# Moving four things in a layer's order of instructions: h's low parts, later column sums, the values' parts, and two stores

## The chip, the cores and the metric

The kernel runs on one core of a Trainium2 chip. The metric is the device time of one launch in microseconds (us); it is measured in several runs, and one execution was profiled besides. The engines are called PE (TensorE), DVE (VectorE), ACT (ScalarE), POOL (GpSimd) and SP (SyncE, which here issues DMA transfers).

## The reference

One layer of a diffusion transformer over 2048 rows of 1024, with 256 rows of context. Everything is fp32.

```python
h  = _modulate(_rmsnorm(x, norm1_g), sh1, sc1)      # h * (1 + sc1) + sh1
hc = _modulate(_rmsnorm(xc, norm1_g), csh1, csc1)
rq, rk, rv, rg, aq, ak, av = jnp.split(h @ w_in, SPLIT_IDX, axis=-1)
...
ret, _, _ = _bidir_retention(rq_h, rk_h, _heads(rv, RET_HEADS), log_gamma, s_f, s_b)
ret = _ret_out(ret, rg, ret_gn_g)                   # norm, then a gate of silu(rg)
...
att = _latent_attention(q..., k, v, kc, vc)         # 8 heads of 64, 2 heads of keys and values
x = x + g1 * (jnp.concatenate([ret, att], axis=-1) @ w_out)
h2 = _modulate(_rmsnorm(x, norm2_g), sh2, sc2)
x = x + g2 * _sqrelu_mlp(h2, w_ff1, w_ff2)
return _rmsnorm(x, final_norm_g)
```

The retention runs over 16 chunks of 128 rows, forwards and backwards: `state = state * c_dec + (k * k_dec)^T v`. The six vectors sh1 to g2 are 1024 wide each and come from `silu(c) @ w_mod + b_mod`.

## The kernel before

Each fp32 product on PE is made of three fp16 products. An operand is split in a high part, rounded by ACT, and a low part, the difference, by DVE; line 645 multiplies high by high, line 646 high by the weights' low part, line 647 h's low part by the weights' high part.

All of it is one program for five engines with manual order: nothing is reordered behind the author's back, each engine works through its own list, and semaphores make it wait for the others. The order is set by a plan. `at(q, step, fn, ...)` puts a function into half-slot q of the first stage, at one of eight steps, and at the end the plan is emitted half-slot by half-slot, step by step:

```python
STEPS = ("dma", "mm", "turn", "copy", "work", "mix", "extra", "store")
```

A slot is one row tile of 128 rows times one chunk of columns of `w_in`, half a slot is half of it: twelve matmuls of 128x128 by 128x512. The chunks come in the order retention values (rv), retention keys (rk), attention keys and values, attention queries, gates (rg, some 435 to 523 us), retention queries (rq, the last chunk, some 523 to 640 us). `rg` and `rq` also name the first half-slots of these chunks. After that come attention and the output projection (to some 1620 us), whose plan `on(k, phase, fn)` is of the same kind, and last the feed-forward part.

What the change touches:

- In the first chunk h is made tile by tile and half by half: PE transposes (`turn_h`, line 461, tile `psx`, two buffers in PSUM), DVE multiplies by the scale (`modulate`, line 466) and POOL adds the shift (line 467), ACT rounds (`high_h`, line 471), DVE subtracts (`low_h`, line 475). Beside it DVE norms later tiles (line 452) and builds the decay tables (lines 973 to 980).
- `later_rows` makes the vectors that are needed later (gates 1 and 2, shift and scale 2). Slices of `w_mod` are loaded (`wmr`), DVE adds them up weighted into `macc` (lines 381 and 383; one buffer), and PE sums over the partitions with a matrix of ones into `mps` (`sums`, line 388; one buffer). `biases` loads `b_mod`, `whole` adds it.
- `value_parts` finds the greatest attention value (lines 770 to 774), writes it per partition to DRAM and reads it back as a row for all partitions (lines 777 and 780), makes a power of two of it (lines 784 to 789), and splits the values with it (lines 793 to 795).
- `ff_scales` finds in the same manner the scales of the feed-forward part (write line 852, read line 855, `scales` lines 859 to 883, `down_scales` lines 888 to 895, then the output's).
- `forward_states(c, q)` makes the forward state of chunk c. SP loads keys and values (line 1007, two buffers), POOL weighs the keys (line 1012), PE multiplies (`product`, line 1018, in the buffer that `mps` has too), DVE adds to the old state (`update`, line 1027), SP stores. They stand at `rq + 4 + c * 29 // 16`, so most products are two half-slots apart, and 5 and 6, and 10 and 11, are one apart.
- `output_tile(t, ...)` adds the projection to a row tile of x, ACT sums its squares (line 1476), `store_x` stores it (line 1479), POOL norms it in place (line 1489), and PE transposes it (line 1494). The tiles run from 15 down to 0, so t = 1 and t = 0 are the last.

Beside DVE's part in the last chunk stands the rotation of the queries (lines 678 and 693). DMA transfers of all queues share eight rotating semaphores, so a transfer is issued only when the transfer eight before it has landed.

Of the kernel before, what the change touches and what calls it, by code (L numbers as in the profile page):

```python
# [55 lines left out]
def layer_kernel(ctx: ExitStack, tc: tile.TileContext, a: dict, out: bass.AP):  # L56
    nc = tc.nc
# [27 lines left out]
    def scratch(name, n, shape, dtype=F32):  # L85
        return [dram.tile(shape, dtype, name=f"{name}{i}", tag=f"{name}{i}") for i in range(n)]
# [13 lines left out]
    x1_d = scratch("x1", NT, [P, D])  # L100
# [161 lines left out]
    with ExitStack() as st:  # L262
# [26 lines left out]
        def at(q, step, fn, *args):  # L289
            plan.setdefault((q, step), []).append((fn, args))  # L290
# [73 lines left out]
        def later_rows(j, use, qs):  # L364


            x = {}

            def load(i, k):
                w = x[i, k] = sg.tile([P, 2, 512], F32, name="wmr", tag="wmr")  # L370
                src = a["w_mod"][0, k * P : (k + 2) * P, (j + i) * 512 : (j + i + 1) * 512]
                nc.sync.dma_start(w, src.rearrange("(k p) n -> p k n", p=P))

            def add(i, k):
                w = x.pop((i, k))
                if k == 0:
                    x["acc"] = one.tile([P, 512], F32, name="macc", tag="macc")
                for r in range(2):
                    c, acc = cc[:, k + r, :1], x["acc"]
                    if k + r == 0:  # L380
                        nc.vector.tensor_scalar_mul(acc, w[:, r], c)
                    else:
                        nc.vector.scalar_tensor_tensor(acc, w[:, r], c, acc, op0=ALU.mult, op1=ALU.add)

            def sums(i):
                if i == 0:
                    x["ps"] = psM.tile([P, 512], F32, name="mps", tag="mps", bufs=1)
                mm(x["ps"][32 * i : 32 * i + 32], ones, x["acc"], start=True, stop=True)

            def biases():  # L390
                b = x["b"] = op.tile([P, 512], F32, name="mrow", tag="xs", bufs=3)
                for i in range(2):
                    src = a["b_mod"][0, (j + i) * 512 : (j + i + 1) * 512]
                    nc.sync.dma_start(b[32 * i : 32 * i + 32], src.partition_broadcast(32))

            def whole():
                nc.vector.tensor_tensor(x["b"][:64], x["ps"][:64], x["b"][:64], op=ALU.add)

            for n, q in enumerate(qs):
                i, k = n // 4, n % 4 * 2  # L400
                at(q - 3, "dma", load, i, k)
                at(q, "extra", add, i, k)
                if k == KT - 2:
                    at(q + 1, "turn", sums, i)
            at(q, "store", biases)
            at(q + 3, "work", whole)
            use(x, q + 4)

        def store_gate(r):
            def store(x):  # L410
# [66 lines left out]
        def first_turn(m):  # L477

            return 2 * m - (3 if m < 4 else 4 if m < 8 else 5 if m < 12 else 6)

        for m in range(2, len(TILES)):
            q = first_turn(m)
            if m > 3:
                at(max(0, first_turn(m - 4) + 2 if m > 5 else 0), "dma", load_x, m)
            if m > 2:
                at(max(0, q - 3), "copy", squares, m)
                at(max(0, q - 2), "work", root, m)
                at(max(1, q - 1), "mix", normal, m)
            for p in range(2):
                at(q + p, "turn", turn_h, m, p)  # L490
                at(q + p + 1, "work", modulate, m, p)
                at(q + p + 2, "copy", high_h, m, p)
                at(q + p + 2, "copy", low_h, m, p)

        class Weights:

# [259 lines left out]
        def value_parts(q0):  # L756

            x = {}

            def load():  # L760
                nc.vector.memset(wv[:, :, :, HD : HD + 1], 1.0)
                for i in range(3):
                    x[i] = xp.tile([P, 2, 6, HD], F32, name="vn", tag="x")
                    nc.sync.dma_start(x[i], av_d[:, :, 6 * i : 6 * i + 6])
                w = xp.tile([P, P + 8], F32, name="vma", tag="x")
                x["m"], x["r"], x["s"], x["e"] = w[:, :P], w[:, P : P + 4], w[:, P + 4 : P + 5], w[:, P + 5 : P + 6]

            def greatest(i):
                v = x[i].rearrange("p g k d -> p (g k d)")
                nc.vector.tensor_reduce(  # L770
                    x["r"][:, i : i + 1], v, axis=AX.X, op=ALU.max, apply_absolute_value=True
                )
                if i == 2:
                    nc.vector.tensor_reduce(x["r"][:, 3:], x["r"][:, :3], axis=AX.X, op=ALU.max)

            def write():
                nc.sync.dma_start(vm_d, x["r"][:, 3:])

            def read():
                nc.sync.dma_start(x["m"], vm_d.partition_broadcast(P))  # L780

            def scale():
                e = x["e"]
                nc.vector.tensor_reduce(e, x["m"], axis=AX.X, op=ALU.max)
                nc.vector.tensor_scalar_max(e, e, 1e-30)
                nc.vector.tensor_single_scalar(e.bitcast(I32), e.bitcast(I32), 0x7F800000, op=ALU.bitwise_and)
                nc.vector.reciprocal(x["s"], e)
                nc.vector.tensor_scalar_mul(x["s"], x["s"], 8192.0)
                nc.vector.tensor_scalar_mul(inv, e, 2.0**-13)

            def parts(i):
                w, v = wv[:, :, 6 * i : 6 * i + 6], x[i]
                nc.vector.tensor_scalar_mul(v, v, x["s"])
                nc.scalar.activation(w[:, :, :, :HD], v, AF.Copy)
                nc.vector.tensor_tensor(w[:, :, :, HD + 1 : VW], v, w[:, :, :, :HD], op=ALU.subtract)

            at(q0, "dma", load)
            for i in range(3):
                at(q0 + 5 + 2 * i, "extra", greatest, i)
                at(q0 + 18 + 2 * i, "extra", parts, i)  # L800
            at(q0 + 10, "store", write)
            at(q0 + 12, "store", read)
            at(q0 + 16, "extra", scale)

        def maxima(i, q):

# [244 lines left out]
        rk, akv, aq, rg, rq = (base[c] for c in (C_RK, C_AKV, C_AQ, C_RG, C_RQ))  # L1051
        row_slots = [rk + 2 * i + 1 for i in range(18)] + [rg + 2 * i + 1 for i in range(14)]
        for n, (j, use) in enumerate(
            ((4, store_gate(0)), (6, turned(shift2)), (8, turned(scale2)), (10, store_gate(1)))
        ):
            later_rows(j, use, row_slots[8 * n : 8 * n + 8])
        big = [rk + 2 * i for i in range(18)] + [rg + 2 * i for i in range(14)]
        sums = [rk - 8 + 2 * i for i in range(4)] + [akv + 2 * i for i in range(18)]
        sums += [aq + 2 * i + 1 for i in range(16)] + [rg + 28, rg + 30]
        for n, q in sorted(enumerate(big + sums), key=lambda x: x[1]):  # L1060
            maxima(n, q)
        decay_tables(8, rq)
        value_parts(rg + 2)
        ff_scales(rq + 5)
        states = {}
        for c in range(NK - 1):
            forward_states(c, rq + 4 + c * 29 // 16)
# [368 lines left out]
    def output_tile(t, k, last):  # L1436
        y = {}
# [38 lines left out]
            nc.scalar.activation(junk, y["x"][:, c], AF.Square, accum_out=y["ss"][:, n : n + 1])  # L1476

        def store_x():
            nc.sync.dma_start(x1_d[t], y["x"])

        def root():
            ss = y["ss"]
# [41 lines left out]
        on(made, "early", add, 1)  # L1524
        on(made, "cast", square, 1)
        on(made + 1, "dma", store_x)
        on(made + 1, "late", root)
        on(made + 4, "late", norm)
# [4 lines left out]
        for q in range(2):  # L1533
            at = k + (31 if t == 1 else 27) + q
# [297 lines left out]
    with tc.manual_schedule():  # L1832
# [47 lines left out]
        for b in range(2 * NB):  # L1880
            turn, final = b == NB - 1, b == 2 * NB - 1
# [6 lines left out]
            for i, (what, *at) in enumerate(jobs, 0 if b else 4):  # L1888
# [19 lines left out]
                bb, m, n = at  # L1908
# [89 lines left out]
```

## Time and profile before

| | us |
|---|---|
| median of three runs | 2894.8 (2894.68, 2894.8, 2895.82) |
| profiled execution, own time | 2892.31 |
| its span in the trace | 2890.5 |
| VectorE busy | 2107.7 |
| GpSimd busy | 1516.0 |
| ScalarE busy | 1429.3 |

The granted TensorE clock was 0.99 of full speed on the mean. The profile is of one execution. A line such as "L466" is a line of the kernel; an instruction is given as what it writes, an arrow, what it reads. A wait is named with the instruction that waited and, behind the arrow, the instruction that ended the wait. Busy times of the engines overlap; only what the last chain of work waited for is time. The lines themselves stand in the prediction.

### The profile page before, as it was taken

What the parts mean: (1) busy time and instruction counts of PE and PEld (TensorE: products, weight loads), DVE (VectorE), ACT (ScalarE), POOL (GpSimd) and SP (SyncE); (2) the same over time, 40 slices, a digit from 0 to 9 for tenths busy, and PEclk for the clock granted to TensorE, in tenths of its full rate; (3) what the DMA queues carried; (4) which work ended last, traced back from release to release, by engine and by line L of the source; (5) the groups of instructions that cost most, each with busy time, mean ns of one, the idle gap of its engine ahead of it and who ended that gap; (6) DMA issues with size and microseconds to landing.
All of it is one profiled execution on the core that took longest, in us unless ns stands there. A gap on an engine that the chain in (4) does not pass through costs nothing. (4 is left out here: it accounts for less than half of the span.)

```text
span 2890.5 us, 45252 instructions
## 1 busy us (share of the span) xinstructions
PE 2730.6 (94%) x17152; PEld 1454.4 (50%) x17152; DVE 2107.7 (73%) x3324; ACT 1429.3 (49%) x2419; POOL 1516.0 (52%) x1289
## 2 busy tenths in 40 slices
PE   6899999998899999999999799999999999999998
PEld 2445654455566666665665344444444444444443
DVE  4656677558878778877886577777777777777776
ACT  3633762237777777777777233333333333333332
POOL 2523771346757568776777465664443434444432
PEclk9999999999999999999999999999999999999999
DMA  7378768562212213231324622231114411111111
GB/s 257 117 232 287 228 177 255 167 199 77 60 55 70 73 60 94 86 104 58 94 79 144 242 81 71 86 117 59 59 49 152 164 59 59 57 50 48 52 44 59
DMA packets 249656, 323.87 MB, mean 112 GB/s; under 512 B 105111, under 2 KB 156311, under 8 KB 247646
## 3 DMA queue, kind: packets, MB, share of 16 engines
q1 hardware_dynamic: 249438, 320.98, 34.7%
q8 instruction: 135, 2.21, 0.3%
q14 instruction: 83, 0.68, 0.1%
HBM read 249.45 MB, written 71.46 MB: 111 GB/s over the span
## 5 line engine op out<-in xcount | busy, mean ns | idle before, releaser
L180 DVE TENSOR_REDUCE nm<-mp 128x1 f32<-128x512 f32 (+1 forms) x576 | 390.2, 684 | 154.3 <-PE mp L167 123.9
L221 POOL TENSOR_TENSOR plo<-p,phi 128x1024 f16<-128x1024 f32 x160 | 352.0, 2201 | 164.7 <-ACT phi L214 134.1
L210 ACT ACTIVATE p<-st 128x512 f32<-128x512 f32 x576 | 337.8, 597 | 181.0 <-PE st L205 103.8
L1772 PE MATMUL pd<-w2hi,uhi 128*128 128x512 f16 x1024 | 388.5, 379 | 13.5 <-DVE acc L1775 13.4
L1773 PE MATMUL pd<-w2lo,uhi 128*128 128x512 f16 x1024 | 388.5, 379 | 0.6 <-DVE w2lo L72 0.6
L1774 PE MATMUL pd<-w2hi,ulo 128*128 128x512 f16 x1024 | 388.6, 379 | 0.0
L1775 DVE SCALAR_TENSOR_TENSOR acc<-pd,sc,acc 128x512 f32<-128x512 f32 x512 | 366.4, 739 | 5.7 <-PE pd L1774 5.6
L1712 PE MATMUL pu<-hf,w1f 128*128 128x512 f16 x896 | 341.3, 381 | 2.5 <-DVE q L1735 2.0
L1713 PE MATMUL pu<-hf,w1f 128*128 128x512 f16 x896 | 341.2, 381 | 0.0
L1714 PE MATMUL pu<-hf,w1f 128*128 128x512 f16 x896 | 341.0, 381 | 0.0
L214 ACT ACTIVATE phi<-p 128x1024 f16<-128x1024 f32 x288 | 303.9, 1055 | 0.0
L646 PE MATMUL pso<-wlo,h 128*128 128x512 f16 (+1 forms) x816 | 296.1, 363 | 3.4 <-DVE wlo L543 3.4
L645 PE MATMUL pso<-whi,h 128*128 128x512 f16 (+1 forms) x816 | 296.5, 363 | 1.3 <-ACT whi L542 1.3
L647 PE MATMUL pso<-whi,h 128*128 128x512 f16 (+1 forms) x816 | 296.0, 363 | 0.0
L223 DVE TENSOR_TENSOR plo<-p,phi 128x512 f16<-128x512 f32 x256 | 246.1, 962 | 16.4 <-ACT phi L214 15.3
L237 PE MATMUL o<-wv,plo 128*128 128x65 f16 x2304 | 235.4, 194 | 19.7 <-POOL plo L221 10.2
L238 PE MATMUL o<-wv,phi 128*128 128x129 f16 x2304 | 243.1, 221 | 0.0
L237 PEld LDWEIGHTS <-plo 128*128 128x128 f16 x2304 | 206.1, 98 | 65.5 <-POOL plo L221 20.6
L204 PE MATMUL st<-qr,ks 128*128 128x512 f16 x576 | 219.7, 381 | 13.6 <-ACT p L210 12.2
L1724 POOL TENSOR_TENSOR r<-r 128x512 f32<-128x512 f32 x64 | 66.3, 1039 | 295.9 <-ACT r L1723 295.9
L205 PE MATMUL st<-qr,ks 128*128 128x512 f16 x576 | 219.8, 382 | 0.1
L167 PE MATMUL mp<-ks,qr 128*128 128x512 f16 x512 | 196.0, 383 | 22.8 <-DVE nm L180 22.4
(331 smaller groups left out, 5391.1 us busy)
## 6 DMA issues: line engine op xcount, KB each, us to landing
wm<-in_w_ff SPq DMA_DIRECT2D x64, 512.0 KB, 4.8
w1r<-in_w_ff SPq DMA_DIRECT2D x64, 512.0 KB, 4.7
ws<-in_w_ff SPq DMA_DIRECT2D x124, 256.0 KB, 3.3
wmr<-in_w_mod SPq DMA_DIRECT2D x32, 512.0 KB, 5.7
hf<-hp SPq DMA_DIRECT2D x56, 256.0 KB, 3.2
hf<-hf SPq DMA_DIRECT2D x14, 1024.0 KB, 6.9
wst<-in_w_in SPq DMA_DIRECT2D x20, 512.0 KB, 6.9
wm<-in_w_mod SPq DMA_DIRECT2D x32, 256.0 KB, 7.1
```

The lines of the kernel that those rows point to most:

```text
L180: nc.vector.tensor_reduce(dst, src, axis=AX.X, op=ALU.max, negate=True)
L210: nc.scalar.activation(self.p[kt // 2][:, kt % 2], self.s.pop(kt), AF.Exp, scale=HD**-0.5)
L214: nc.scalar.activation(hi, self.p[j], AF.Copy)
L221: nc.gpsimd.tensor_tensor(lo, p, hi, op=ALU.subtract)
L237: mm(o[:, : HD + 1], lo[:, i, c], v[:, : HD + 1], start=False, stop=False)
L1712: mm(pu[i], whi, hi, start=k == 0, stop=False)
L1713: mm(pu[i], whi, lo, start=False, stop=False)
L1714: mm(pu[i], wlo, hi, start=False, stop=k == 3)
L1772: mm(ps, uh, wh, start=f == 0, stop=False)
L1773: mm(ps, uh, wl, start=False, stop=False)
L1774: mm(ps, ul, wh, start=False, stop=f == NF - 1)
L1775: nc.vector.scalar_tensor_tensor(acc[:, c], ps, sc2, acc[:, c], op0=ALU.mult, op1=ALU.add)
```

## The change

```diff
             if k == KT - 2:
-                at(q + 1, "turn", sums, i)
-        at(q, "store", biases)
-        at(q + 3, "work", whole)
-        use(x, q + 4)
+                at(q + 2, "turn", sums, i)
+        at(q + 1, "store", biases)
+        at(q + 4, "work", whole)
+        use(x, q + 5)
...
             at(q + p + 2, "copy", high_h, m, p)
-            at(q + p + 2, "copy", low_h, m, p)
+            at(q + p + 2, "mix", low_h, m, p)
...
         for i in range(3):
-            at(q0 + 5 + 2 * i, "extra", greatest, i)
-            at(q0 + 18 + 2 * i, "extra", parts, i)
-        at(q0 + 10, "store", write)
-        at(q0 + 12, "store", read)
-        at(q0 + 16, "extra", scale)
+            at(q0 + 3 + i, "extra", greatest, i)
+            at(q0 + 11 + i, "extra", parts, i)
+        at(q0 + 5, "store", write)
+        at(q0 + 7, "store", read)
+        at(q0 + 10, "extra", scale)
...
-    value_parts(rg + 2)
-    ff_scales(rq + 5)
+    value_parts(rq + 1)
+    ff_scales(rq + 16)
...
     def store_x():
-        nc.sync.dma_start(x1_d[t], y["x"])
+        (nc.scalar if t < 2 else nc.sync).dma_start(x1_d[t], y["x"])
```

No arithmetic is added or removed. It does four things.

**A.** The low part of h goes from the step "copy" to the step "mix", behind "work" of the same half-slot, where the next `modulate` stands. In VectorE's list in the first chunk, by the decay tables (the difference, - before and + after):

```order
 L973 TENSOR_TENSOR dw<-dw 128x8
 L974 TENSOR_TENSOR lgp<-lgp,dw 128x8
+L466 TENSOR_TENSOR t<-psx,a_237 128x512
 L475 TENSOR_TENSOR h_1081<-t,h_1081 128x512
-L466 TENSOR_TENSOR t<-psx,a_237 128x512
 L452 TENSOR_SCALAR x_l_1025<-x_l_1025,ry_x 128x1024
 L979 TENSOR_SCALAR dw<-rel,lgp 128x128
 L980 SCALAR_TENSOR_TENSOR dw<-rel,lgp,dw 128x128
```

Here `h_1081` is a tile of h, `psx` the transposed x, `dw` a decay table. The multiplication by the scale (line 466) of the next half now stands ahead of the low part (line 475) of the half before; norm and tables stand behind both, as they did.

**B.** The column sums of `later_rows` go one half-slot later, and with them what follows on them. **C.** The values' parts go from the chunk of gates to the last chunk, closer together, and the feed-forward scales eleven half-slots back in the last chunk. PE's list in the chunk of gates, where the last sum leaves its old place and where it comes back, some 25 rows on:

```order
 L647 LDWEIGHTS h_1557
 L647 MATMUL pso<-whi,h_1557 128x512
-L388 MATMUL mps<-macc,ones 32x512
 L167 LDWEIGHTS qr
 L167 MATMUL mp<-ks,qr 128x512
```

```order
 L647 LDWEIGHTS h_1557
 L647 MATMUL pso<-whi,h_1557 128x512
+L388 MATMUL mps<-macc,ones 32x512
 L645 LDWEIGHTS h_1613
 L645 MATMUL pso<-whi,h_1613 128x512
```

It moved behind one more group of twelve matmuls. VectorE's list in the last chunk, ahead of the feed-forward scales (line 859 is the first of them, line 883 the last; lines 678 and 693 are the rotation, line 1027 the update of a forward state):

```order
-L678 TENSOR_TENSOR t_5930<-xs,tb_5821 128x512
+L678 TENSOR_TENSOR t_6244<-xs,tb_6122 128x512
+L693 TENSOR_TENSOR ys<-t_6244,t_6245 128x512
 L1027 SCALAR_TENSOR_TENSOR rst<-rst,cd,mpr 128x128 x4
-L693 TENSOR_TENSOR ys<-t_5930,t_5931 128x512
+L678 TENSOR_TENSOR t_6306<-xs,tb_6191 128x512
 L859 TENSOR_REDUCE fsb<-fs 128x6
 L862 COPY fsb<-fsb 128x4
```

and behind them:

```order
 L882 TENSOR_TENSOR scu<-fsb 128x1
 L883 SCALAR_TENSOR_TENSOR scu<-scu,fsb 128x1
-L678 TENSOR_TENSOR t_6015<-xs,tb_5882 128x512
+L693 TENSOR_TENSOR ys<-t_6306,t_6307 128x512
 L1027 SCALAR_TENSOR_TENSOR rst<-rst,cd,mpr 128x128 x4
-L693 TENSOR_TENSOR ys<-t_6015,t_6016 128x512
+L678 TENSOR_TENSOR t_6391<-xs,tb_6252 128x512
+L1027 SCALAR_TENSOR_TENSOR rst<-rst,cd,mpr 128x128 x4
 L888 TENSOR_REDUCE fsb<-fg 128x1
 L125 TENSOR_SCALAR fsb<-fsb 128x1
```

Before, the scales stood ahead of the update of product 4. Now they stand ahead of that of product 10, and the update of product 11 follows after one step of a rotation.

**D.** The stores of the last two row tiles are issued by ScalarE instead of SP. ScalarE's list at tile 1:

```order
 L1476 ACTIVATE junk,ss<-xr 128x512
 L1650 ACTIVATE w1f<-w1s,sc_242 128x512
+L1479 DMA x_205<-xr 128x1024
 L1740 ACTIVATE v<-pu 128x512
 L1452 ACTIVATE rh<-bank_20787 128x512
```

The transfer stands ahead of the relu of the first feed-forward products (line 1740) and of the high part of a retention tile (line 1452); in SP's list it is gone from behind seven loads of 1 MB (line 1701).

## The prediction

> **What bounds the kernel now.** The first line of the page gives TensorE (PE) 2730.6 us of the profiled span of 2890.5, so the time falls only where PE is idle or runs at a reduced clock. I read next a table by stage for the stretches that the change touches (stretch, length, busy time and count of PE, PEld, DVE, ACT, POOL, granted clock, DMA share, GB/s), then PE's waits.
>
> ```profile
> PE 2730.6 (94%) x17152; PEld 1454.4 (50%) x17152; DVE 2107.7 (73%) x3324; ACT 1429.3 (49%) x2419; POOL 1516.0 (52%) x1289
> 42.00:175.00 133.00, 117.95 (x579) 60.73 (x580) 86.91 (x162) 75.42 (x141) 57.27 (x70) 0.95 0.41 131
> 435.00:523.00 88.00, 81.50 (x366) 35.33 (x365) 65.17 (x103) 24.07 (x45) 18.04 (x14) 0.98 0.78 233
> 523.00:640.00 117.00, 109.31 (x598) 62.16 (x597) 64.48 (x167) 26.24 (x43) 49.69 (x54) 0.99 0.57 184
> 1580.00:1640.00 60.00, 47.12 (x203) 21.89 (x202) 27.30 (x39) 19.00 (x36) 26.27 (x26) 0.89 0.76 284
> ```
>
> In the four stretches (the chunk of retention values, the chunk of gates, the last chunk, the last output tiles) PE is idle for 15, 6.5, 7.7 and 12.9 us. The waits name what ends that idleness (in all, times, longest):
>
> ```profile
> PE bank L1494 <- POOL xr L1489: 13.8, 8, 6.6
> PE psx L461 <- DVE t L466: 9.4, 4, 4.6
> PE mps L388 <- DVE macc L383: 6.5, 3, 4.3
> PE mpr L1018 <- issue: 3.3, 3, 1.6
> ```
>
> Each of them belongs to one part of the change. Together they are 33 us, 1.1% of the time; 0.2%, 5.8 us, is about what a measurement of this kernel can tell from no change. All sums are against the profiled execution's own 2892.3 us; the median of the runs is 2894.8, so I add 2.5 at the end.
>
> **Part A, h's low parts behind the next modulation.** The loop of one half-slot in the first chunk, by the timeline (start, duration, in brackets the idle time before and what ended it), and two of PE's stalls:
>
> ```profile
> 84.92 0.68 DVE L466 TENSOR_TENSOR t<-psx,a 128x512 f32<-128x512 f32 x1
> 85.68 1.48 POOL L467 TENSOR_TENSOR t<-t,s 128x512 f32<-128x512 f32 x1 [1.16 <-DVE t L466]
> 87.19 0.63 ACT L471 ACTIVATE h<-t 128x512 f16<-128x512 f32 x1 [1.30 <-POOL t L467]
> 87.86 0.69 DVE L475 TENSOR_TENSOR h<-t,h 128x512 f16<-128x512 f32 x1 [1.59 <-ACT h L471]
> 88.46 0.68 DVE L466 TENSOR_TENSOR t<-psx,a 128x512 f32<-128x512 f32 x1
> ...
> 89.20 1.12 PE L461 MATMUL psx<-ident,x_l 128*128 128x128 f32 x4 [2.40 <-DVE t L466]
> 118.50 1.12 PE L461 MATMUL psx<-ident,x_l 128*128 128x128 f32 x4 [4.56 <-DVE t L466]
> ```
>
> VectorE (DVE) modulates, GpSimd (POOL) adds the shift, ScalarE (ACT) rounds to the high part, DVE subtracts for the low part, and only then takes the next modulation: 84.92 to 88.46, 3.54 us a turn, while PE's half-slot, twelve matmuls at 0.21 (rows below) and four transposes of some 0.11, takes about 3.0. DVE itself stands idle for 1.59 us before the low part. PE's transposes have two buffers, so PE waits for a modulation once the loop has slipped by a turn or two: 9.4 us in four stalls.
>
> With the low part behind the next modulation, that modulation waits only for its transposes. The chain of one tile half (0.68 + 1.48 + 0.63 + 0.69, about 3.5 us) now spreads over two half-slots, 6 us, which leaves 2.5 us against an added table or norm of 0.3 to 1.5 us in DVE's row. So I take the four stalls as gone: +9.4. Queued behind the moved instruction are DVE's norm of a later tile and its table pieces, each 0.6 us later by one modulation, none awaited by PE within a half-slot. What is late next is the low part itself: PE's third matmul of a group (line 647) needs it, for the first tiles some 1.5 us after it is made and later tiles are turned further ahead; I charge 0.6 us, one modulation once.
>
> After a stall PE is slow for a while. The clock of one stretch, and the matmuls after the stall at 118.50:
>
> ```profile
> 88.00:92.00 4.00, 2.80 (x9) 1.61 (x10) 2.19 (x4) 2.86 (x8) 1.78 (x3) 0.64 0.38 121
> ...
> 119.40 0.63 PE L645 MATMUL pso<-whi,h 128*128 128x512 f16 x1
> ...
> 123.49 0.38 PE L646 MATMUL pso<-wlo,h 128*128 128x512 f16 x1
> 123.70 0.38 PE L647 MATMUL pso<-whi,h 128*128 128x512 f16 x1
> ```
>
> From 119.40 to 123.49 ten matmuls take 4.09 us where ten at 0.21 (123.49 to 123.70) would take 2.1: 2.0 lost, and half of the 0.90 of the transposes ahead, 2.4 together. After 89.20 the granted clock of 0.64 over 4 us costs 1.4. The two shorter stalls I give nothing. Part A: 9.4 + 3.8 - 0.6 = **+12.6** (bounds: 9 if the clock is lost for another reason, 14 if all four stalls cost clock).
>
> The Trainium skill, TensorE: Matmul & The Clock Gate, Part 1 (the HAM clock gate), says that the half clock follows at least one idle window of about 3.4 us. The row differs: the stall of 2.40 us at 89.20 already had it. By that sentence part A would be about 1.4 less, 11.2; the sum goes by the rows.
>
> **Parts B and C in the chunk of gates: sums a half-slot later, values' parts gone.** One stall, and DVE's value work there (count, busy, mean ns, idle before):
>
> ```profile
> 512.91 1.91 PE L388 MATMUL mps<-macc,ones 128*32 128x512 f32 x2 [4.34 <-DVE macc L383]
> L795 DVE TENSOR_TENSOR wv<-vn,wv 128x768 f16<-128x768 f32 x3 | 2.9, 961 | 2.7 <-ACT wv L794 2.7
> L770 DVE TENSOR_REDUCE vma<-vn 128x1 f32<-128x768 f32 x3 | 2.8, 947 | 0.0
> L793 DVE TENSOR_SCALAR vn<-vn,vma 128x768 f32<-128x768 f32 x3 | 1.8, 610 | 0.0
> 512.00:516.00 4.00, 3.09 (x6) 0.69 (x7) 1.42 (x3) 0.00 (x0) 0.00 (x0) 0.57 1.00 346
> ```
>
> The column sum (line 388) waits for DVE's last weighted addition. 2.9 + 2.7 + 2.8 + 1.8, and about 1.2 for the eight small ones, is 11.4 us of DVE's row taken out of 88 in which it was busy for 65; and the sum is asked for a half-slot later, 2.75 us (88 us over 32). The longest wait, 4.34, is less than the two together, so all 6.5 go. The clock of 0.57 over 4 us at 512 costs 1.7, part of it the stall itself; I take 1.4. One new wait: the first addition of the next group (line 381) overwrites what the sum reads, so DVE stands behind PE for up to 1 us; I take 0.9 off, since DVE has 20 us to spare there: **+7.0** (bounds 4 and 8.5). The three loads and the two small transfers by way of DRAM leave SP's row here; nothing of PE waits for them.
>
> **Part C in the last chunk.** The products of the forward states (line 1018) share one PSUM buffer, so product c+1 waits for DVE's update of c (line 1027). The feed-forward scales (lines 859 to 883) stand in DVE's row between them:
>
> ```profile
> 559.87 1.05 PE L1018 MATMUL mpr<-rkv,rkw 128*128 128x128 f32 x8
> 560.78 1.53 DVE L859 TENSOR_REDUCE fsb<-fs 128x6 f32<-128x768 f32 x1 [3.76 <-DMA fs<-smd]
> 566.23 0.16 DVE L883 SCALAR_TENSOR_TENSOR scu<-scu,fsb 128x1 f32<-128x1 f32 x1
> 566.91 1.11 DVE L1027 SCALAR_TENSOR_TENSOR rst<-rst,cd,mpr 128x128 f32<-128x128 f32 x4
> ...
> 568.13 1.13 PE L1018 MATMUL mpr<-rkv,rkw 128*128 128x128 f32 x8 [1.59 <-issue]
> 573.36 1.13 PE L1018 MATMUL mpr<-rkv,rkw 128*128 128x128 f32 x8 [1.07 <-POOL rkw L1012]
> 599.47 1.06 PE L1018 MATMUL mpr<-rkv,rkw 128*128 128x128 f32 x8
> 603.49 1.13 PE L1018 MATMUL mpr<-rkv,rkw 128*128 128x128 f32 x8 [0.37 <-issue]
> ```
>
> Before, the scales run from 560.78 to 566.39 and the products at 568.13 and 573.36 wait for 1.59 and 1.07. After, the scales stand eleven half-slots later, and the value parts (0.61 + 0.96 + the wait for ACT, 2.5 us each) stand where those products are. They are spread over three half-slots and stand behind the update or just ahead of it: the first wait goes and a third of the second stays, **+2.0** (bounds 0 and 2.7).
>
> The new place of the scales is bad: the products 10 and 11, at 599.47 and 603.49, are one half-slot apart (most others are two), and the scales now stand between the start of product 10 and its update. Their data comes by a read that SP issues behind a load for product 12, which waits for product 10's start; I take it to land 0.9 us after that start, as the same read did before, behind a load for product 6 (product 4 at 559.87, the scales at 560.78). Then 0.9 + 5.6 (scales) + 0.7 (rotation) + 1.1 (update) = 8.3 us until product 11 may start, against 4.0 now: a new stall of 4.3, and 2.1 of clock behind it, between the 1.4 and the 2.4 of part A: **-6.4** (bounds -8, with a clock loss as at 118.50, and 0, if the scales' data is there 4 us earlier and they run in DVE's idle time).
>
> **Part D, the last two rows' stores by ScalarE's queue.** Transfers (first the issue on SP, x7 of 1 MB in a row) and who waits:
>
> ```profile
> 1568.72 12.48 SPq L1701 DMA_DIRECT2D hf<-hf x7
> 1587.34 0.32 SPq L1479 DMA_DIRECT2D x<-xr x1
> ...
> 1587.98 0.71 ACT L1650 ACTIVATE w1f<-w1s,sc 128x512 f16<-128x512 f32 x1
> ...
> DMA to landing us min/median/max: 2.7/2.8/11.5
> ...
> 1599.06 1.12 POOL L1489 TENSOR_SCALAR xr<-xr,cy_f 128x1024 f32<-128x1024 f32 x1 [8.59 <-DMA x<-xr]
> 1600.23 1.12 PE L1494 MATMUL bank<-ident,xr 128*128 128x128 f32 x4 [6.55 <-POOL xr L1489]
> ...
> 1626.39 1.11 PE L1494 MATMUL bank<-ident,xr 128*128 128x128 f32 x4 [3.87 <-POOL xr L1489]
> ```
>
> POOL's norm writes over x, so it waits until the store has landed: 11.5 us for tile 1, behind seven loads of 1 MB on the same queue, against a median of 2.8. On ACT's queue the store stands behind ACT's last square and a weight conversion, so it is issued at 1588.7, some 1.4 us later, and it shares the 16 DMA engines with what is left of the loads. If nothing were ahead of it, it would land at 1588.7 + 2.8 = 1591.5 and PE's 6.55 would go; if it fared as before, at 1588.7 + 11.5 = 1600.2, 1.4 later than now. I take the middle, 1595.9, since half of the engines' time would be its own: +2.9 for tile 1. For tile 0, two small loads and the store go together and the wait of 3.87 is cut by less, +1.6. Sum **+4.5** (bounds -1 and +15, with both waits, 10.4, and some 4.6 of clock, the windows' deficit of 0.11 over 60 us being 6.6). ACT may stand at the issue while an earlier load of the same semaphore lands, and behind it ACT's relu and the high parts of the next product; PE would then idle sooner in the same gap, which I cost at nothing as long as the store lands last.
>
> **Sum.** 12.6 + 7.0 + 2.0 - 6.4 + 4.5 = 19.7 less: 2892.3 - 19.7 = 2872.6, and 2.5 more against the median: **2875**.
>
> **Rivals.**
> No stall at product 11 (the scales' data is early, or the update overtakes): 6.4 less, 2868.7. For it: DVE is busy for only 64.48 of 117 us; against: the order is fixed.
> Both gaps of the output tiles go: 4.5 becomes 15, 2864.6. For it: the median landing of 2.8; against: a DMA share of 0.76 there.
> Half of part A stays, because the decay tables between modulations still hold DVE: 6.3 more, 2881.4. For it: the longest stall, 118.50, stands among the tables in DVE's row.
> The store gains nothing on the other queue: 4.5 more, 2879.6. The loads and the store use the same 16 engines, which were busy to 0.76 in that stretch, and the 11.5 us behind seven loads suggest that what was issued first is served first. The Trainium skill, DMA: Bandwidth & Descriptors, Issuing engines are not separate DMA queues, says just that: another engine's issue saves the time to initiate only. No run here shows it.
> No change: the low part becomes what PE waits for in the first tiles. Part A's 12.6 isn't gained, and nine turns lose the 0.6 of one modulation each, 5.4: 2893. For it: DVE was busy for 87 of 133 us there and has little room in a turn; against: tiles are turned ahead of their use.
> Slower: in the last chunk the DVE row of moved work (11.4 of values, 5.6 and 2.9 of scales, 20 us) falls wholly between updates and products, so that PE pays for it, and seven stalls, from product 5 to 11, cost some 1.6 of clock each, 11: 31 in the place of 6.4 gives 2868.7 + 31 = 2900. It decides from 26 us lost there; against it stand 52 us of DVE's idle time in that chunk.
>
> **Chances.** The forecast, by itself 2871 to 2880: 0.48. No stall at 11: 0.15. Both gaps: 0.09. Half of A: 0.10. Store for nothing: 0.09. No change: 0.05. Slower: 0.04. The range 2864 to 2885 takes in all but the last two. Faster by over 0.2% (below 2889): 0.91; within: 0.05; slower: 0.04.
>
> **What would show it.** Right: no wait of line 461 for line 466 in the first chunk and a granted clock near 1 there; none of line 388 for line 383 in the gates; one of line 1018 of 4 to 5 us near 585 to 600, behind line 883; the waits of line 1494 for line 1489 at some 3.5 and 2 us. Wrong would be: a wait of line 647 for line 475; a larger sum of waits of line 1018; stores with a landing as long as now, or ACT's line 1740 held at its DMA.

## The result and the profile after

The changed kernel took 2881.26 us (median of four runs, 2877.23 to 2882.76) against 2895.31 of the kernel before (2894.68 to 2898.38): a ratio of 0.9947, 95% interval 0.9930 to 0.9964. The forecast was 2875. It is faster and inside the range, but 6 us slower than the sum said: just above the 2871 to 2880 that the forecast claimed for itself, and at the 2881.4 of the rival that half of part A stays. The experiments show that A came nearly whole and the time went elsewhere, so the number alone would have pointed to the wrong rival. The profiled execution took 2882.76, the slowest of its four; its span is 2881.0.

The page's first line, three of the stages of the prediction (same columns; since everything now lies 9 to 20 us earlier, the cuts no longer fall on the same instructions), and PE's waits:

```profile
PE 2732.5 (95%) x17152; PEld 1455.9 (51%) x17152; DVE 2119.7 (74%) x3324; ACT 1430.4 (50%) x2419; POOL 1524.2 (53%) x1289
```

```profile
42.00:175.00 133.00, 126.57 (x634) 65.09 (x635) 98.37 (x170) 76.83 (x143) 63.50 (x70) 0.97 0.51 164
435.00:523.00 88.00, 88.00 (x415) 40.32 (x414) 60.45 (x87) 26.06 (x50) 24.59 (x20) 1.00 0.65 208
523.00:640.00 117.00, 102.94 (x555) 59.79 (x554) 72.99 (x185) 30.66 (x49) 46.78 (x50) 0.94 0.61 187
```

```profile
PE bank L1494 <- POOL xr L1489: 11.8, 9, 5.2
...
PE mpr L1018 <- issue: 8.3, 3, 4.4
...
PE bank L1447 <- DVE rl L1454: 2.8, 1, 2.8
...
PE mpr L1018 <- POOL t L681: 2.0, 1, 2.0
PE psx L461 <- DVE t L466: 2.0, 2, 1.2
```

The wait for modulation is 2.0 instead of 9.4. That of line 388 is gone, and the gates' chunk is dense. The last chunk lost 14 us of PE time instead of 7.7, at a clock of 0.94. The waits for the stores fell by 2 us only, and a new one of 2.8 stands beside them.

What each stage is worth is read best from marks: the first and last start of one line's matmuls, before and after. The first two rows are the kernel before:

```profile
L1018 PE MATMUL mpr<-rkv,rkw x136: 272/276/348, 536.9 to 633.2; 128*128 128x128 f32 x136
L1772 PE MATMUL pd<-w2hi,uhi x1024: 376/379/380, 1632.2 to 2877.4; 128*128 128x512 f16 x171
```

and these the changed kernel:

```profile
L1018 PE MATMUL mpr<-rkv,rkw x136: 272/275/550, 516.9 to 623.5; 128*128 128x128 f32 x136
L204 PE MATMUL st<-qr,ks x576: 376/379/634, 629.6 to 1559.5; 128*128 128x512 f16 x192
L1772 PE MATMUL pd<-w2hi,uhi x1024: 376/379/379, 1621.7 to 2867.9; 128*128 128x512 f16 x171
```

The first product of a forward state comes 20.0 us earlier: the gain of the first chunk and of the gates together. From the first to the last of these products it takes 106.6 us instead of 96.3: 10.3 given back in the last chunk. The last line 204 stood at 1568.3 before; from there to the first line 1772 it takes 62.2 us instead of 63.9, so the stores brought 1.7. Attention and feed-forward, which the change doesn't touch, are longer by 0.8 and 1.0.

The start of product 7, first before and then after, divides the last chunk:

```profile
579.94 1.06 PE L1018 MATMUL mpr<-rkv,rkw 128*128 128x128 f32 x8
563.62 1.06 PE L1018 MATMUL mpr<-rkv,rkw 128*128 128x128 f32 x8
```

From the first product to product 7 it takes 46.8 us instead of 43.1 (front, 3.7 lost), and from there to the last 59.0 instead of 52.5 (back, 6.6 lost).

The last chunk, by the timeline (products on PE, then what DVE and SP did):

```profile
542.68 1.13 PE L1018 MATMUL mpr<-rkv,rkw 128*128 128x128 f32 x8 [2.66 <-issue]
...
555.38 2.03 PE L1018 MATMUL mpr<-rkv,rkw 128*128 128x128 f32 x8 [2.03 <-POOL t L681]
...
591.24 2.04 PE L1018 MATMUL mpr<-rkv,rkw 128*128 128x128 f32 x8 [4.36 <-issue]
...
540.86 0.69 DVE L678 TENSOR_TENSOR t<-xs,tb 128x512 f32<-128x512 f32 x1 [10.36 <-DMA tb<-in_ret_cs]
541.47 1.12 DVE L1027 SCALAR_TENSOR_TENSOR rst<-rst,cd,mpr 128x128 f32<-128x128 f32 x4
...
584.57 1.53 DVE L859 TENSOR_REDUCE fsb<-fs 128x6 f32<-128x768 f32 x1 [0.41 <-DMA fs<-smd]
...
529.35 0.38 SPq L777 DMA_DIRECT2D vm<-vma  x1
...
530.34 0.41 SPq L660 DMA_DIRECT2D tb<-in_ret_cs  x1
...
534.84 4.83 SPq L1007 DMA_DIRECT2D rkv<-rv  x1
```

Product 11 (591.24) waits 4.36 behind the scales, as foreseen. Two others were not: product 4 (542.68) and product 6 (555.38). At 540.86 DVE has been waiting 10.36 us for a table of the rotation that SP issued at 530.34, one microsecond after it had issued the write of the values' maxima (line 777), and the update that product 4 waits for stands behind it. SP itself was held for 4.83 us at the second issue behind that table. In the kernel before, the same write and the read that waits for its landing stood ten us apart in the chunk of gates:

```profile
463.49 0.46 SPq L777 DMA_DIRECT2D vm<-vma  x1
...
473.43 0.33 SPq L780 DMA_DIRECT2D vma<-vm  x1
```

The DMA engines in the changed kernel from 534 to 539 us (share 0.78, but 20 GB/s), and the granted clock (the third figure from the end) around product 4 and behind product 6:

```profile
534.00:539.00 5.00, 5.00 (x29) 2.65 (x28) 0.00 (x0) 1.18 (x2) 0.00 (x0) 1.00 0.78 20
540.00:548.00 8.00, 5.34 (x32) 3.25 (x32) 6.74 (x18) 1.18 (x2) 5.75 (x6) 1.00 0.77 247
555.00:562.00 7.00, 6.62 (x27) 3.87 (x28) 4.27 (x10) 2.02 (x3) 1.21 (x2) 0.76 0.50 165
```

And the output tiles: ScalarE's issue of the store, what it held, PE's gaps, and the landing of line 1479 (least, median, greatest):

```profile
1581.77 0.35 ACTq L1479 DMA_DIRECT2D x<-xr  x1
1582.17 0.60 ACT L1740 ACTIVATE v<-pu 128x512 f32<-128x512 f32 x1 [2.24 <-DMA hf<-hf]
...
1584.03 0.66 PE L1447 MATMUL bank<-ident,ma 128*128 128x128 f32 x4 [2.76 <-DVE rl L1454]
...
1589.10 1.12 POOL L1489 TENSOR_SCALAR xr<-xr,cy_f 128x1024 f32<-128x1024 f32 x1 [7.38 <-DMA x<-xr]
1590.27 1.12 PE L1494 MATMUL bank<-ident,xr 128*128 128x128 f32 x4 [2.99 <-POOL xr L1489]
...
1616.96 1.12 PE L1494 MATMUL bank<-ident,xr 128*128 128x128 f32 x4 [5.21 <-POOL xr L1489]
```

```profile
DMA to landing us min/median/max: 2.8/2.9/8.0
```

ScalarE reached the store at 1579.93, after the conversion of line 1650, and issued it at 1581.77, when one of the hf loads had landed. The high part that PE's next product needs came that much later. The landing of 8.0 is that of tile 0's store; tile 1's, issued at 1581.77, had landed when GpSimd's norm began at 1589.10, after some 7.3.

### The profile page after: what moved, and what is told of

The parts are those of the page before. It is cut to its first block, busy times and chain, and to the rows that moved or that the text cites. A ratio compares the mean times of both kernels' runs of the same rounds, so it can differ in the third digit from the quotient of the medians.

```text
span 2881.0 us, 45242 instructions
## 1 busy us (share of the span) xinstructions
PE 2732.5 (95%) x17152; PEld 1455.9 (51%) x17152; DVE 2119.7 (74%) x3324; ACT 1430.4 (50%) x2419; POOL 1524.2 (53%) x1289
## 5 line engine op out<-in xcount | busy, mean ns | idle before, releaser
L1772 PE MATMUL pd<-w2hi,uhi 128*128 128x512 f16 x1024 | 388.0, 379 | 12.6 <-DVE acc L1775 12.4
L204 PE MATMUL st<-qr,ks 128*128 128x512 f16 x576 | 220.3, 382 | 14.9 <-ACT p L210 13.3
```

The lines of the kernel that those rows point to most:

```text
L1772: mm(ps, uh, wh, start=f == 0, stop=False)
```

## The experiments

Each was timed against the kernel before; where two experiments are compared, it is by their ratios, and by marks in their traces. The runs of one kernel mostly lie within some 3 us of their median, a few 8 or 9 away, so small differences of medians tell nothing by themselves.

**A alone.** The edit is the one line `at(q + p + 2, "mix", low_h, m, p)` in the kernel before.

> The kernel before with part A alone: h's low part behind the next modulation, nothing else. Theory (A's sum holds): no wait of line 461 for line 466 over 1.5 us, granted clock near 1 in the first chunk, the three waits of line 388 for line 383 (6.5 us) still there; 12 to 13 us less than before, about 2882.5. Rival (half of A stays, because of the decay tables): 6 us less, about 2889.

Measured 2885.34 us, ratio 0.9953 (0.9938 to 0.9968). PE's waits:

```profile
PE mps L388 <- DVE macc L383: 6.6, 3, 5.0
PE mpr L1018 <- POOL t L681: 3.3, 1, 3.3
...
PE psx L461 <- DVE t L466: 2.0, 2, 1.2
```

The mark of the first column sum is at 184.6 us instead of 196.6: A brought 12.0 in the first chunk, the forecast was 12.6, and the median is 12.7 under that of the kernel before in the same series (2897.99). The rival falls: its 6 us lie outside the interval, and 7.4 of the 9.4 us of waiting are gone. The profiled execution kept 9.9 (2882.46 against 2892.31). Part of what is missing is the last chunk, untouched here, which takes 98.4 us instead of 96.3: behind the scales product 5 (558.70) waits 3.3 instead of 1.6 and a slow clock follows, while product 6 waits no longer. The chunk's waits shift when it starts at another time; in the next experiment the same 3.3 stands there.

**A and B.** A alone, and the four lines of `later_rows` from the change; values' parts, scales and stores as before.

> The kernel before with parts A and B alone: h's low part behind the next modulation and the column sums a half-slot later, the values' parts left in the chunk of gates. Theory (the half-slot of 2.75 us covers most of the waits of line 388; the longest, some 4.5, needs the values' work gone too): the waits of line 388 for line 383 fall from 6.6 us to between 1 and 3, the write of 4-byte pieces holds up the transfers in the chunk of gates, where PE does not wait for them, and the last chunk has the short waits of before: 4 to 6 us less than A alone, about the same as the changed kernel. Rival (the sums go on waiting, since DVE falls behind by more than a half-slot): no less than A alone.

Measured 2883.41, ratio 0.9952 (0.9940 to 0.9965). One wait of line 388 is left:

```profile
PE mps L388 <- DVE macc L383: 3.0, 1, 3.0
```

The size of the wait is as expected: 3.6 us of waiting went. The forecast of 4 to 6 us beyond A alone failed: the ratios are the same, as the rival's time has it, though not for its reason. By the marks B is worth 3.0. (The first product comes at 524.6 against 525.7 in A alone, but this execution began the first chunk 1.9 late, its first line 461 on x at 57.4 against 55.5.) A and B alone are about as fast as the whole change. So C and D together brought nothing that the times can tell: what C brought in the gates (first product 524.6 to 516.9, 5.9 without the late beginning) went again in the last chunk, where A and B alone take 98.5 us from the first to the last product and the whole change 106.6.

**The maxima in 16 bytes per partition.** What product 4 waits for is disputed: the write itself, or DVE's work.

```diff
-    vm_d = dram.tile([P], F32, name="vm", tag="vm")
+    vm_d = dram.tile([P, 4], F32, name="vm", tag="vm")
...
-                nc.sync.dma_start(vm_d, x["r"][:, 3:])
+                nc.sync.dma_start(vm_d, x["r"])
...
-                nc.sync.dma_start(x["m"], vm_d.partition_broadcast(P))
+                nc.sync.dma_start(x["m"], vm_d.rearrange("p a -> (p a)").partition_broadcast(P))
```

> The changed kernel with the values' maxima written to DRAM as 16 bytes per partition instead of 4 (four columns, all of them read back; the greatest is the same). Theory: the write of 128 pieces of 4 bytes holds up all transfers for some 5 us, so that the rotation's table lands 10.4 us after its issue and product 4 waits for 2.66 us; with 16 bytes the table lands within 4 us, the wait of product 4 goes, and that of product 6 (2.03, and its slow clock) shrinks: 3 to 6 us less than the changed kernel, 2875 to 2878. Rival 1 (any write of 128 small pieces holds up the transfers, or something else does at that time): landing and waits as now, 2881. Rival 2 (the write is quick but product 4 waits for DVE's value work): 1 us less.

Measured 2880.46, ratio 0.9943 (0.9928 to 0.9957). The same place in the trace (from line 778 on this kernel's lines are one further), and the DMA engines over five microseconds, as long behind the write as in the window above:

```profile
536.22 0.69 DVE L678 TENSOR_TENSOR t<-xs,tb 128x512 f32<-128x512 f32 x1 [4.20 <-DMA tb<-in_ret_cs]
...
536.37 0.42 SPq L1008 DMA_DIRECT2D rkv<-rv  x1
...
541.39 1.05 PE L1019 MATMUL mpr<-rkv,rkw 128*128 128x128 f32 x8
```

```profile
535.50:540.50 5.00, 5.00 (x28) 2.68 (x28) 2.42 (x6) 0.36 (x1) 2.94 (x3) 1.00 0.65 199
```

Product 4 (541.39) has no wait, SP is not held at the second load of line 1008 (0.42), and the engines move 199 GB/s where they moved 20. The table landed 4.3 us after its issue, not quite within 4. The edit enlarges the read back as well, but in the changed kernel the read was issued only at 540.24, behind the microseconds in which the transfers stood still, so it did not cause them. So the write of 128 pieces of 4 bytes is what holds the transfers up here; rival 1 falls, and with the wait of product 4 rival 2. The wait of product 6 shrank little, from 2.03 to 1.82, but no slow clock follows it. From first to last product it takes 101.0 us instead of 106.6, 4.8 of it in the front. The medians do not show it (0.8 us less; the intervals overlap).

**The scales elsewhere.**

```diff
-            at(q0, "dma", load)
+            at(q0 + 1, "dma", load)
...
-        ff_scales(rq + 16)
+        ff_scales(rq + 13)
```

> The changed kernel with the feed-forward scales three half-slots earlier (from half-slot 13 of the last chunk, the loads one later), so that they stand behind the update of product 8 with two half-slots until product 9's. Theory (the scales between products 10 and 11 cost 6.4): the wait of 4.36 at product 11 goes and no other of line 1018 grows over 1 us: about 6 us less than the changed kernel, 2875. Rival (DVE's 5.6 us of scales delay whichever product comes next): a wait of 2 to 4 us at product 9 or 10, 2878 to 2881.

Measured 2876.80, ratio 0.9930 (0.9916 to 0.9943). From first to last product it takes 100.6 us, 6.0 less than in the changed kernel, and the longest wait of line 1018 is that of product 6:

```profile
PE mpr L1018 <- issue: 2.9, 2, 1.6
PE mpr L1018 <- POOL t L681: 2.0, 1, 2.0
...
PE mpr L1018 <- POOL rkw L1012: 1.9, 1, 1.9
```

The rival falls, since products 9 and 10 have no wait. The theory holds in part. The wait for the scales is gone, but product 11 still waits, 1.9 us for the weighed keys, where the theory had nothing:

```profile
586.72 1.13 PE L1018 MATMUL mpr<-rkv,rkw 128*128 128x128 f32 x8 [1.88 <-POOL rkw L1012]
```

And only 3.4 of the 6.0 lie in the back, where the scales stood. The other 2.7 lie in the front: product 4 waits 1.6 instead of 2.7, ahead of anything that was moved, and no slow clock follows product 6. That 6.0 comes near the 6.4 is luck.

**Both repairs.** The two edits above together.

> The changed kernel with both repairs of the last chunk: the values' maxima written as 16 bytes per partition, and the feed-forward scales three half-slots earlier. Theory (the two losses are apart and add up, 3 to 5 us and 6 us): the only wait of line 1018's products over 1 us is that of product 6, about 2; 2870 to 2873. Rival (the two meet in DVE's row, one repair gives back what the other gains): 2876.

Measured 2873.35, ratio 0.9919 (0.9906 to 0.9933). First to last product 98.1 us. That is 8.5 less than the changed kernel, and 8 by the medians (2881.26). The 5.6 and 6.0 of the two experiments are 11.6 and do not add up to it, since each has some of the other's stretch in it. Front and back of the last chunk (starts of line 1018's products, as above) tell them apart:

| kernel | front, us | back, us |
|---|---|---|
| before | 43.1 | 52.5 |
| changed | 46.8 | 59.0 |
| stores on SP (below) | 45.2 | 58.3 |
| norm apart (below) | 46.7 | 58.9 |
| 16 bytes | 42.0 | 58.2 |
| scales moved | 44.1 | 55.6 |
| both repairs | 43.7 | 53.5 |
| all three (below) | 42.3 | 54.1 |

The second to fourth differ only behind this chunk and show how far one order scatters. The fronts with the 4-byte write are 44.1 to 46.8, those with 16 bytes 42.0 to 43.7; the backs with the scales in the new place are 58.2 to 59.0, with the scales moved 53.5 to 55.6. The groups do not overlap, though in the front by little: on the mean the write is worth some 3 us and the place of the scales some 4. Waits of 1.4 at product 11 and 1.3 at the last product are there beside the 1.9 of product 6, a little more than expected.

**The stores back on SP's queue.** `nc.sync.dma_start(x1_d[t], y["x"])` for all tiles in the changed kernel.

> The changed kernel without part D: all stores of x on SP's queue again. Theory (D gains little: in the changed kernel's trace the two waits of line 1494 are 8.2 us against 10.4 before, and ScalarE held at the store's issue gives PE a new wait of 2.8 for line 1454): the waits of line 1494 are 10 to 11 us again, that of line 1447 for line 1454 is 0.4 again, and the time is the same within 2 us, 2880 to 2883. Rival (D's forecast of 4.5 us): 2886.

Measured 2883.53, ratio 0.9954 (0.9941 to 0.9968), which is not told apart from the changed kernel. PE's wait for the norm, and the landing of line 1479:

```profile
PE bank L1494 <- POOL xr L1489: 13.6, 8, 5.6
```

```profile
DMA to landing us min/median/max: 2.8/2.9/10.6
```

The wait of line 1447 for line 1454 is 0.4 again. From the last line 204 to the first line 1772 it takes 63.8 us, against 62.2 with D and 63.9 before. D is worth 1.6 us at that place; the same stretch takes 61.2 to 61.7 in the three other kernels with D and the norm in place, and 62.8 and 63.9 in A alone and in A and B.

**The norm apart.** In the changed kernel the norm of tiles 1 and 0 is written to two half buffers of its own, which the transposes then read.

```diff
-            nc.gpsimd.tensor_scalar(y["x"], y["x"], y["r"], 1.0, op0=ALU.mult, op1=ALU.mult)
+            if t > 1:
...
+            y["n"] = [xp.tile([P, 512], F32, name="xn", tag="xn", bufs=1), xp.tile([P, 512], F32, name="xm", tag="u")]
+            for i in range(2):
+                half = y["x"][:, i * 512 : (i + 1) * 512]
+                nc.gpsimd.tensor_scalar(y["n"][i], half, y["r"], 1.0, op0=ALU.mult, op1=ALU.mult)
...
```

> The changed kernel with the norm of the last two row tiles written to buffers of its own, in two halves, instead of over x, so that it doesn't wait for the store of x. Theory (PE's gaps at the last two tiles are the stores' landing): the two waits of 2.99 and 5.21 us and the slow clock behind them go, 9 to 12 us less than the changed kernel, 2869 to 2872. Rival (without the store's wait PE meets the next one, for loads that share the DMA engines or for ScalarE behind its held issue): half of it, 2876.

Measured 2878.38, ratio 0.9934 (0.9920 to 0.9949): 3 us by the medians, not 9 to 12, and the intervals overlap. Both waits for the norm are gone. These came:

```profile
1608.72 0.72 ACT L1657 ACTIVATE w1f<-w1r,sc 128x512 f16<-128x512 f32 x1 [2.71 <-DMA g2b<-gs]
```

```profile
PE pd L1779 <- ACT w2hi L71: 3.1, 1, 3.1
PE bank L1447 <- DVE rl L1454: 3.0, 1, 3.0
PE pd L1780 <- DVE w2lo L72: 2.1, 3, 0.9
```

The rival was right in its size and in its second way. ScalarE is held at its two store issues until an earlier transfer has landed (before the instruction behind the second it stood idle for 2.71 us, the issue included), and PE meets what ScalarE hadn't done. The first feed-forward product (line 1779, the 1772 of the others) comes 9.0 us earlier than in the changed kernel, 1612.7, the last only 2.7 earlier: the products of line 1779 take 1252.5 us from first to last. With the stores on SP's queue, in the next experiment, they take 1245.9, which points to the held ScalarE for those 6.3. That loads had a part in it is not shown.

**All three.** Both repairs, the norm apart, and the stores on SP's queue again.

> Both repairs of the last chunk, and the norm of the last two row tiles in buffers of its own with the stores on SP's queue again, so that ScalarE is not held at their issue. Theory: the waits of the transposes for the norm and that of line 1447 for line 1454 are both gone, PE's waits at the last two tiles fall from 14 us to under 4, and some of it is given back to loads in the first feed-forward products: 4 to 7 us less than with the two repairs alone, 2864 to 2868. Rival (PE then waits for the same loads a little later): 1 us less, 2870.

Measured 2866.78, ratio 0.9897 (0.9883 to 0.9910).

```profile
PE bank L1501 <- POOL xn L1496: 4.1, 1, 4.1
```

As the theory had it, 6.6 us less than the two repairs alone. PE's waits from 1560 to 1650 us sum to 10.1 where they were 14.9 with the two repairs, not the "under 4" that was expected (that stretch has some first feed-forward products in it). What is left is a wait of 4.1 for the last tile's norm, whose chain on GpSimd now comes late behind the weights' sums, no longer behind a store.

**The values' parts earlier.**

```diff
-                at(q0 + 11 + i, "extra", parts, i)
+                at(q0 + (11, 13, 14)[i], "extra", parts, i)
...
-        value_parts(rq + 1)
+        value_parts(rq - 3)
```

> The kernel with both repairs of the last chunk and the norm apart, and the values' parts four half-slots earlier, over the end of the gates' chunk, with the three pieces behind the updates of products 2, 3 and ahead of that of 4, so that none stands between products 5 and 6. Theory (product 6 waits for 2 us because three pieces of 2.5 us stand in DVE's row around products 5 and 6, which are one half-slot apart): no wait of line 1018 over 0.7 us, and no new wait of line 388: 2 to 4 us less, 2863 to 2865. Rival (the tight pair waits anyway, for GpSimd's weighed keys or the rotation): a wait of 1 to 2 us at product 6 stays, 2866.

Measured 2863.78, ratio 0.9894 (0.9875 to 0.9912).

```profile
582.60 1.13 PE L1018 MATMUL mpr<-rkv,rkw 128*128 128x128 f32 x8 [1.79 <-POOL rkw L1012]
611.50 1.13 PE L1018 MATMUL mpr<-rkv,rkw 128*128 128x128 f32 x8 [1.30 <-issue]
```

These two are the only waits of the products from 560 us on, and before that there is none: product 6 has no wait. First to last product takes 94.7 us against 97.3, less than the kernel before's 96.3, and the front 39.9, less than in any other kernel. So the values' work was what held product 6 up; the edit moves their maxima and transfers too, so it does not single out the three pieces. The waits of 1.79 and 1.30 were there already (1.67 and 1.31), so "none over 0.7" was too much. By the ratios it is not told apart from the kernel of the last experiment; it has the lowest median here, 1.1% under the kernel before.

## Why the prediction came out as it did

- **Part A** (+12.6): right. 12.0 by the mark of the first sum in A alone, 11.2 by that of the first product. The waits of line 461 fell from 9.4 to 2.0, 7.4 us; part of the rest came with the clock, which rose from 0.95 to 0.97 over the 133 us of that stretch. The two waits that are left, 1.24 at 110 and 0.78 at 118, stand among the decay tables; so that rival had a point, but a small one.
- **The gates** (+7.0): right in its mechanism and a little low; the 8.8 lie above its bound of 8.5. First chunk and gates together gave 20.0 where 19.6 was forecast, 11.2 of it A's, so 8.8 in the gates: 3.0 by the half-slot, 5.9 by taking the values' work out. The new wait of DVE for the sum (line 381) was 5.9 us there in three times, the longest 2.3, not up to 1 as put. No wait of PE for DVE's sums came of it, so the 0.9 taken off for it was not needed.
- **Last chunk, front** (+2.0): the step that failed. It said that the first wait goes and a third of the second stays. Measured: waits of 2.66 (product 4) and 2.03 (product 6) in the place of 1.59 (product 5) and 1.07 (product 6), and a clock of 0.76 over the 7 us from 555, 1.7: 3.7 us lost, as by the marks, where 2.0 were to be gained. Two things were missed. The write of the maxima was moved along at no cost, though it was a transfer that SP had been stalled behind in the trace of before (landed after 9.9 us there, in the chunk of gates, where nothing of PE waited for it); in the last chunk a table, and behind it the forward state, was queued behind it. With 16 bytes the front was on the mean some 3 us shorter. And three value parts of 2.5 us each, put at a third of the second wait, held product 6 up: with the values' work moved away, its wait was gone and the front 2 to 4 us shorter than in the other kernels with 16 bytes.
- **Last chunk, back** (-6.4): right. A stall of 4.36 at product 11 (4.3 forecast, and against 0.37 before) and a slow clock behind it: product 12 comes 9.1 us after product 11 instead of 6.6, 2.5 lost where 2.1 was put. That is 6.5, and 6.6 by the marks. Moving the scales three half-slots gave only some 4 of it back, since product 11 then waits for the weighed keys.
- **Part D** (+4.5): mis-sized, 1.7 by the marks and 1.6 by undoing it. Tile 1's store went as put: it landed after some 7.3 us (7.2 put), and the wait fell from 6.55 to 2.99, 3.6 where 2.9 was put. But ScalarE was held at the issue until an hf load had landed, which the prediction named and costed at nothing: PE's wait for line 1454 grew from 0.4 to 2.76. And tile 0's store, put at +1.6, landed after 8.0 and its wait grew from 3.87 to 5.21. The rival that the other queue saves next to nothing was the nearest. The Trainium skill (DMA: Bandwidth & Descriptors, Issuing engines are not separate DMA queues) says that transfers started by different engines share the same 16 DMA engines and that another engine's issue saves only the time to initiate. The landings of 7.3 and 8.0 us, far from the undisturbed 2.9, agree with it; with the stores on SP's queue they were 10.6 and 6.5.
- Sum: 20.0 - 10.3 + 1.7, less 1.8 in stages that the change does not touch: 9.6 us between the two profiled executions. The medians differ by 14.0, since the profiled execution of after is the slowest of its four and that of before lies under all timed runs shown with it. By the two traces the change is worth half of the 19.7 that was forecast, so the median's nearness to 2875 owes something to that scatter. What sets it was not tried.
- Two of the prediction's own signs of being wrong came: the waits of line 1018 grew, from 4.4 to 10.3 in all (the forecast's own terms, 4.3 more and 2.0 less, made it some 7), and ScalarE's line 1740 was held at its transfer.

## What to carry to other kernels

When a step moves, its transfers move: look in the old place for how long each took to land and what stood behind it on its queue, since a slow one that nobody waited for there can stand ahead of something urgent in the new place. Work that is taken out of one dense stage is not free in the next one if a single PSUM buffer ties product and update to each other; put it right behind an update that has the longest way to the next product. To free a buffer that a store holds, a second buffer (6.6 us, with the stores back on SP's queue) was worth more than a second queue (1.6).

## What the hardware showed

- A write of 128 pieces of 4 bytes to 512 bytes of DRAM held up all transfers of the core: 20 GB/s over 5 us some 5 us behind its issue, a following table landing after 10.4 us, SP held 4.83 us at an issue. With 16 bytes per partition, 2 KB, the same stretch had 199 GB/s, the table landed after 4.3 us, and SP's issues near it took at most 1.4 us in the four kernels with the larger write. In the kernel before, where the write stood in the chunk of gates, it landed after 9.9 us too. Why the small pieces do it was not tried.
- A stall of 2.66 us at product 4 was followed by no slow matmul (granted clock 1.00 over 540 to 548), while one of 2.03 at product 6 was (0.76 over 555 to 562), and one of 2.40 in the trace before. In the kernel with the stores back on SP's queue a stall of 2.43 at product 4 was followed by slow matmuls (product 5 came 8.25 us later instead of 6.6). The length of a stall alone does not tell whether clock is lost.
